# A hybrid attention and mLSTM encoder layer: another order of the attention unit's steps, and four more pieces of dense products at the start of each attention stage

## The chip, the core and the metric

The kernel runs on one NeuronCore of a Trainium2 chip. A core has a matrix engine (TensorE, "PE" in the profile; its weight loads are "PEld"), VectorE ("DVE"), ScalarE ("ACT"), GpSimd ("POOL") and SyncE ("SP"), which here mostly issues DMAs. Each engine works through its own instructions in order and waits on semaphores for the others. The metric is device time in microseconds (us) of one execution of the whole program. The kernel before takes 2937.11 us (median of 3 runs, 2936.93 to 2938.26).

## What is computed

One encoder layer over two sequences (1024 and 2048 tokens, each with 16 learned meta tokens in front), model width 1024, in 32-bit floating point:

```python
xn = _rmsnorm(h, g_pre)
proj = xn @ w_in + b_in                      # 1024 -> 6672 columns
na_q, na_k, na_v, na_z, ml_qk, ml_v, ml_z, ml_o, ml_g, mg = jnp.split(proj, SPLIT_IDX, axis=-1)
ya = _neighbourhood_attention(...)           # 8 heads of 64, window of 8 rows x 16 columns, plus meta keys
ya = (ya * jax.nn.silu(na_z)) @ w_a
yb = (_mlstm_branch(...) * jax.nn.silu(ml_z)) @ w_b   # 4 heads of 128, both directions
ga, gb = jnp.split(jax.nn.sigmoid(mg), 2, axis=-1)
y = (ga * ya + gb * yb) @ w_out
return h + _rmsnorm(y, g_post)
```

In the neighbourhood attention each block of queries (8 rows by 16 columns, 128 queries) sees the keys of up to 15 rows by 32 columns and the meta keys; a bias table and a mask give each query its own window:

```python
s_win = jnp.einsum('bcqhd,bwckhd->bhcqwk', q_blk, k_blk) * scale
s_win = jnp.where(valid[:, :, None, :], s_win + bias, NEG)
s_met = jnp.einsum('bcqhd,bmhd->bhcqm', q_blk, km) * scale
p = jax.nn.softmax(jnp.concatenate([s_met, s_win], axis=-1), axis=-1)
```

## The kernel before

Large products are made of three products of 32-bit values cut into a high and a low half (high times high, high times low, low times high: `mm3`, lines 141 to 146). The cutting is work for ScalarE (the high half is a rounding copy) and VectorE (the low half is the difference); the text calls it splitting.

**Two streams.** `dense` is a generator for the input projection (`group`, lines 412 to 414 for the token-major columns, 144 to 146 for the feature-major ones), and for the six "finals" of 512 tokens each (`final`): the merge of the two branches with `w_a`, `w_b` (lines 144 to 146 on `yh`, `yl`) and `w_out` (lines 1304 to 1306). `sparse` is a generator for the rest: mLSTM of the first sequence, attention of the first sequence, mLSTM of the second, attention of the second. `run` weaves them: each `yield` of the sparse stream carries a cost (`A_NA` = 1.52 for attention), and `run` takes pieces from the dense stream until their costs (about 1.4 each: 12 matmuls of 256 columns or 6 of 512) have paid for it. So a `yield` in the sparse stream puts about one piece of dense products into TensorE's order. When the sparse stream has ended, the remaining pieces follow without anything between. A dense final for which an attention or mLSTM result is still missing may not start. There are 1642 pieces. The first attention stage begins at piece 449, the second at 1142 and ends at 1567; the last final begins at 1578.

TensorE's order is the order of this program text. The order on the other engines and of SyncE's DMA issues is chosen by a scheduler at build time.

**An attention stage** (`na`) walks over heads (a block of 8 rows, and one of 8 heads; 16 in the first stage, 32 in the second), and in each over 4 units `cb`, the blocks of 16 columns. For each unit there are four steps:

- `na_scores`: two matmuls on TensorE (lines 664, 665) into the one PSUM buffer `sc`; VectorE adds the bias and takes the maximum (668); ScalarE takes the exponential (672).
- `na_scale`: VectorE takes a reciprocal and scales the probabilities (680, 681), tile `prb`, 2 buffers.
- `na_turn`: four transposes on TensorE (689) into one of 2 PSUM buffers `tr`; ScalarE copies the high half (691), VectorE the low half (692), tile `pts`, 2 buffers.
- `na_out`: four matmuls with v on TensorE (701) into one of 2 PSUM buffers `sm`; ScalarE and VectorE add up the result (705, 707), and after the last unit of a pair of heads multiply it with the gate (709) and store it in HBM (710, tile `ya`).

These are spread over iterations of a loop: iteration `u` issues the scores of unit `u`, the product with v of unit `u - 2` and the transposes of unit `u - 1`, with a `yield` behind each.

`na_prep` loads and splits what the next head needs, in six parts: the DMA loads (`qr`, `kr`, `vr`, and so on, lines 550 and 629 to 633), then the splits of q (639, 641, 642), of k (644, 646) and of v (649, 651). In the loop these parts are called one by one between the steps. For the first head of a stage nothing runs ahead, so its six parts are called before the loop, with a `yield` behind each.

**The finals.** `yload` (lines 1245 to 1248) loads the eight pieces of 128 features of a final's input from HBM, four from attention (`ya`) and four from mLSTM (`yb`), through four buffers, and splits each (1247 on ScalarE, 1248 on VectorE). It is called in parts from the final before, as soon as the attention and mLSTM results are there; what is left of it is called at that final's end. The gates of the merge (`tg`, line 1267) are loaded for each block of features and multiplied on VectorE straight out of PSUM (1283, 1285), which sets free the accumulators `pj` (3 buffers). Weights come through four pairs of buffers, `whi` and `wlo` (line 231); the next pair's loads are issued when a pair is used up.

Of the kernel before, what the change touches and what calls it, by code (L numbers as in the profile page):

```python
# [48 lines left out]
def _row_types(R):  # L49

    out = []
    for t in range(R // 8):
        if t == 0:
            out.append((0, 0, 11))
        elif t == R // 8 - 1:
            out.append((2, R - 12, 12))
        else:
            out.append((1, 8 * t - 4, 15))
    return out
# [48 lines left out]
A_NA, A_D, A_A, A_N, A_G = 1.52, 1.63, 1.63, 1.85, 1.3  # L108


class K:
# [440 lines left out]
    def na(self, s, rts):  # L552

        tc, nc, i = self.tc, self.nc, self.i
        rows = _row_types(SEQLEN[s] // 64)
        with tc.tile_pool(name=f"na{s}{rts[0]}", bufs=1, side="right", reuse_waits="tile") as np_:
            self.qB = [np_.tile([P, 4, P], F32R, name=f"qB{j}") for j in range(2)]
            self.kx = [np_.tile([P, 16, 64], F32R, name=f"kx{j}") for j in range(2)]
            self.gts = [np_.tile([P, 17, 48], F32, name=f"gt{j}") for j in range(2)]
            for q in self.qB:  # L560
                nc.gpsimd.dma_start(q[64:128], i["onehot"].rearrange("a (b c) -> a b c", b=4))
            for g in self.gts:
                nc.gpsimd.memset(g[:, 0, :], 0.0)
                nc.gpsimd.memset(g[:, 16, :], 0.0)
            heads = [(rt, pr, hh) for rt in rts for pr in range(4) for hh in range(2)]
            n = len(heads)
            prep = self.na_prep(np_, s, rows, heads, 0)
            for k in range(6):
                next(prep, None)
                yield A_NA  # L570
            self.na_bias(rows, heads, 0)
            cur, nxt = self.head, None
            units = [(j, cb) for j in range(n) for cb in range(4)]
            ready = {}
            for u in range(len(units) + 2):
                if u < len(units):
                    j, cb = units[u]
                    if cb == 0:
                        cur = self.head
                        prep = self.na_prep(np_, s, rows, heads, j + 1) if j + 1 < n else iter(())  # L580
                        next(prep, None)
                    ready[u] = [cur, heads[j], cb, None, None, self.gts[j % 2]]
                    self.na_scores(np_, ready[u], rows)
                    if j + 1 < n and cb == 0:
                        self.na_bias(rows, heads, j + 1)
                yield A_NA
                if u < len(units):
                    self.na_scale(np_, ready[u])
                    if cb:
                        next(prep, None)  # L590
                if u >= 2:
                    self.na_out(np_, ready.pop(u - 2), s)
                yield A_NA
                if 1 <= u <= len(units):
                    self.na_turn(np_, ready[u - 1], rows)
                    if u < len(units) and cb >= 2:
                        next(prep, None)
                yield A_NA

    def na_bias(self, rows, heads, j):  # L600
# [892 lines left out]
```

## Time and profile before

| what | us |
|---|---|
| median of 3 runs | 2937.11 |
| profiled execution, device time | 2935.2 |
| its span, first to last instruction | 2933.4 |
| TensorE busy in the span | 2820.8 |
| first attention stage, first scores to last product with v | 794.6 to 1183.5 |
| second attention stage, likewise | 2024.5 to 2810.9 |
| last final, first matmul | 2829.5 |

All times in the text are counted from the start of the span. In the profile `out<-in` names the tiles that an instruction writes and reads, `x4` is a count, and a bracket at a line's end gives the idle time of the engine ahead of that instruction and what ended it. In tables of waits the three numbers are the total, how often, and the longest. In views by stretches each engine has its busy time and its number of instructions, and the last three columns are the granted clock of TensorE (1.00 is full), the busy share of the DMA engines and GB/s. In the chain of waits the columns are start, length and what ran.

### The profile page before, as it was taken

The page shows a single profiled execution, that of the slowest core. Times are in us where ns is not written, and L with a number is a line of the kernel's source. Part 1 is how long each engine was busy: PE and PEld are TensorE (multiplying, and loading weights), DVE is VectorE, ACT ScalarE, POOL GpSimd, SP SyncE. Part 2 cuts the span into 40 slices and gives each one's busy share as a digit, 9 for nine tenths or more (in the row PEclk, how much of TensorE's full clock was granted, in tenths as well). Part 3 has the DMA queues.
Part 4 walks back from the last instruction along what each step waited for, and adds up shares of the span by engine and source line. Part 5 has one row for each costly group of instructions (what it writes and reads, how often), then busy time and mean ns, then how long its engine had stood idle before and what let it go on. Part 6 is the DMA issues. An engine that isn't in the chain of part 4 may idle for free.

```text
span 2933.4 us, 49345 instructions
## 1 busy us (share of the span) xinstructions
PE 2820.8 (96%) x17488; PEld 2510.8 (86%) x17488; DVE 1747.6 (60%) x4722; ACT 1288.7 (44%) x3114; POOL 23.1 (1%) x107
## 2 busy tenths in 40 slices
PE   6999999999799999999999999989999999989998
PEld 6998898899689988888887998977888888879797
DVE  5233566556556665465568776565555557777843
ACT  4213546433344444456566554413444445435421
POOL 1000000000000000000000000000000000000000
PEclk9999999999899999999999999999999999999999
DMA  9655667656775654568679898488568658897875
GB/s 350 219 179 181 197 218 256 232 182 207 255 232 153 198 175 134 168 232 298 197 234 363 277 313 290 136 263 272 172 196 283 191 174 272 245 280 236 283 273 194
DMA packets 438760, 675.25 MB, mean 230 GB/s; under 512 B 52240, under 2 KB 253024, under 8 KB 438512
## 3 DMA queue, kind: packets, MB, share of 16 engines
q1 hardware_dynamic: 437392, 669.41, 70.1%
q0 software_dynamic: 1120, 2.69, 0.4%
q8 instruction: 137, 2.24, 0.3%
q14 instruction: 111, 0.91, 0.1%
HBM read 455.05 MB, written 216.90 MB: 229 GB/s over the span
## 4 chain that ended last, share of the span: by engine, by line
PE 83%; DMA 9%; DVE 5%; ACT 1%; issue 1%; SPq 1%; DVEq 0%; ACTq 0%
PE pj L144 15%; PE pj L145 15%; PE pj L146 15%; PE pj L412 6%; PE pj L413 6%; PE pj L414 6%; PE sm L701 3%; PE pj L1304 3%; PE pj L1306 3%; PE pj L1305 3%; PE tr L689 2%; DMA tg<-gt 2%; PE sc L665 1%; PE sc L664 1%; PE sm L146 1%; PE sm L145 1%
## 5 line engine op out<-in xcount | busy, mean ns | idle before, releaser
L144 PE MATMUL pj<-xh,whi 128*128 128x512 f32 (+1 forms) x1824 | 722.2, 396 | 2.4 <-DVE xl L310 2.2
L145 PE MATMUL pj<-xl,whi 128*128 128x512 f32 (+1 forms) x1824 | 701.3, 384 | 0.6 <-DVE xl L310 0.6
L146 PE MATMUL pj<-xh,wlo 128*128 128x512 f32 (+1 forms) x1824 | 699.8, 384 | 0.0
L412 PE MATMUL pj<-whi,xh 128*128 128x256 f32 (+3 forms) x1576 | 450.8, 286 | 0.0
L413 PE MATMUL pj<-wlo,xh 128*128 128x256 f32 (+3 forms) x1576 | 444.7, 282 | 0.0
L414 PE MATMUL pj<-whi,xl 128*128 128x256 f32 (+3 forms) x1576 | 444.2, 282 | 0.0
L146 PEld LDWEIGHTS pj<-xh,wlo 128*128 128x128 f32 x1824 | 344.6, 189 | 72.3
L144 PEld LDWEIGHTS pj<-xh,whi 128*128 128x128 f32 x1824 | 345.2, 189 | 57.3 <-DVE xl L310 2.6
L145 PEld LDWEIGHTS pj<-xl,whi 128*128 128x128 f32 x1824 | 345.9, 190 | 53.3 <-DVE xl L310 0.8
L412 PEld LDWEIGHTS pj<-whi,xh 128*128 128x128 f32 (+1 forms) x1576 | 294.3, 187 | 1.2
L413 PEld LDWEIGHTS pj<-wlo,xh 128*128 128x128 f32 (+1 forms) x1576 | 294.0, 187 | 1.1
L414 PEld LDWEIGHTS pj<-whi,xl 128*128 128x128 f32 (+1 forms) x1576 | 294.1, 187 | 0.9
L692 DVE TENSOR_TENSOR pts<-tr,pts 96x512 fp32r<-96x512 f32 (+2 forms) x192 | 132.2, 688 | 159.4 <-ACT pts L691 158.3
L672 ACT ACTIVATE prb<-sc,mx 128x384 f32<-128x384 f32 (+2 forms) x192 | 119.4, 622 | 238.2 <-DVE mx L668 234.1
L1304 PE MATMUL pj<-whi,mh 128*128 128x256 f32 x768 | 221.0, 288 | 0.4 <-DMA whi<-wh 0.4
L1306 PE MATMUL pj<-whi,mlo 128*128 128x256 f32 x768 | 217.6, 283 | 2.1 <-DVE mlo L1287 2.1
L1305 PE MATMUL pj<-wlo,mh 128*128 128x256 f32 x768 | 217.2, 283 | 0.0
L691 ACT ACTIVATE pts<-tr 96x512 fp32r<-96x512 f32 (+2 forms) x192 | 114.3, 595 | 170.0 <-PE tr L689 169.3
L421 DVE TENSOR_TENSOR stT<-pj,bb 128x256 f32<-128x256 f32 (+3 forms) x197 | 83.1, 422 | 145.3 <-PE pj L414 141.2
L144 PE MATMUL pj<-yh,whi 128*128 128x512 f32 x384 | 158.0, 412 | 11.0 <-DVE tg L1283 11.0
L668 DVE CUSTOM_DVE_ANT_1 sc<-sc,gt 128x384 f32<-128x384 f32 (+2 forms) x192 | 118.9, 619 | 73.2 <-PE sc L665 67.4
L146 PE MATMUL pj<-yh,wlo 128*128 128x512 f32 x384 | 153.4, 399 | 0.0
(234 smaller groups left out, 5067.5 us busy)
## 6 DMA issues: line engine op xcount, KB each, us to landing
whi<-wh SPq DMA_DIRECT2D x176, 512.0 KB
wlo<-wl SPq DMA_DIRECT2D x176, 512.0 KB
wh<-whi SPq DMA_DIRECT2D x64, 512.0 KB
wl<-wlo SPq DMA_DIRECT2D x64, 512.0 KB
wraw<-w_in SPq DMA_DIRECT2D x48, 512.0 KB
gt<-st SPq DMA_DIRECT2D x96, 256.0 KB
tg<-gt SPq DMA_DIRECT2D x96, 256.0 KB
xh<-xh SPq DMA_DIRECT2D x6, 2048.0 KB
```

The source lines that it names most:

```text
L144: mm(out, ah, bh, start=start, stop=False)
L145: mm(out, ah, bl, start=False, stop=False)
L146: mm(out, al, bh, start=False, stop=stop)
L412: nc.tensor.matmul(o, xh, wh, start=k == 0, stop=False)
L413: nc.tensor.matmul(o, xh, wl, start=False, stop=False)
L414: nc.tensor.matmul(o, xl, wh, start=False, stop=k == KT - 1)
L668: nc.vector.tensor_tensor_reduce(out=so, in0=so, in1=gt[:, g0:g0 + ns, c0:c0 + 32], op0=ALU.add, op1=ALU.min, scale=-1.0, scalar=3.0e38, a ...
L672: nc.scalar.activation(pr_[:, :N].rearrange("p (b a c) -> p b a c", b=4, c=8), sc[:, :N].rearrange("p (a b c) -> p b a c", b=4, c=8), AF.E ...
L692: nc.vector.tensor_tensor(pts[:ks, :, 1, :], pt[:ks], pts[:ks, :, 0, :].bitcast(F32), op=ALU.subtract)
L1304: nc.tensor.matmul(o, mh[:, k, xs], wh, start=k == 0, stop=False)
L1305: nc.tensor.matmul(o, mh[:, k, xs], wl, start=False, stop=False)
L1306: nc.tensor.matmul(o, ml[:, k, xs], wh, start=False, stop=k == KT - 1)
```

## The change

In the loop of `na`, the transposes of unit `u - 1` move from the third step to the second, ahead of whose `yield` they now stand, behind the scaling of unit `u`; the product with v of unit `u - 2` moves from the second step to the third. The second part of `na_prep` in an iteration keeps its place in the third step. The first of the six parts before the loop, the one with the loads, is followed by five `yield`s instead of one; this holds for both attention stages.

```diff
             for k in range(6):
                 next(prep, None)
-                yield A_NA
+                for _ in range(1 if k else 5):
+                    yield A_NA
...
                     self.na_scale(np_, ready[u])
                     if cb:
                         next(prep, None)
+                if 1 <= u <= len(units):
+                    self.na_turn(np_, ready[u - 1], rows)
+                yield A_NA
                 if u >= 2:
                     self.na_out(np_, ready.pop(u - 2), s)
-                yield A_NA
-                if 1 <= u <= len(units):
-                    self.na_turn(np_, ready[u - 1], rows)
-                    if u < len(units) and cb >= 2:
-                        next(prep, None)
+                if u < len(units) and cb >= 2:
+                    next(prep, None)
                 yield A_NA
```

With it the second attention stage begins at piece 1146 and ends at piece 1575 of the dense stream; the last final still begins at 1578. From line 571 on the changed kernel's lines stand one lower: line 701 is 702 there, and so on.

## The prediction

> **What bounds the kernel now.** I read the engines' shares first, then the waits of TensorE, then the stretches in which attention runs, then the queues around its two ends.
>
> ```profile
> span 2933.4 us, 49345 instructions
> PE 2820.8 (96%) x17488; PEld 2510.8 (86%) x17488; DVE 1747.6 (60%) x4722; ACT 1288.7 (44%) x3114; POOL 23.1 (1%) x107
> ```
>
> TensorE is the bound: it is busy for 2820.8 of 2933.4 us. The change issues the same matmuls, so only the 112.6 us in which TensorE stands still can shrink or grow. The table of TensorE's waits (total, times, longest) says which of them attention owns:
>
> ```profile
> PE sm L701 <- DVE pts L692: 15.7, 12, 4.7
> PE sc L664 <- ACT kd L644: 15.0, 2, 14.1
> ...
> PE pj L1304 <- DMA whi<-wh: 0.4, 1, 0.4
> ```
>
> L701 is the product with v, waiting for the second half of the split of the transposed probabilities. L664 is the first score of an attention stage, waiting for the split of its loads. The transposes (L689) never wait, as the groups by line show (the last column is idle time before them):
>
> ```profile
> L701 PE MATMUL sm<-pts,vt 96*128 96x256 f32 (+2 forms) x768 | 124.2, 284 | 16.0 <-DVE pts L692 15.7
> L689 PE MATMUL tr<-ident,prb 128*96 128x128 f32 (+2 forms) x768 | 115.8, 274 | 0.0
> ```
>
> **Part 1, the order within a unit step.** Between two steps TensorE gets a piece of dense products. An undisturbed stretch of the chain of waits gives its length:
>
> ```profile
> 2539.98 0.44 PE tr L689 x4
> ...
> 2541.87 0.23 PE sc L664
> 2542.10 0.23 PE sc L665
> ...
> 2543.76 0.47 PE sm L701 x4
> ```
>
> From the end of the transposes (2540.42) to the scores are 1.45 us, from the scores' end (2542.33) to the product with v 1.43 us. So a piece is 1.43 us, scores take 0.46, transposes 0.44, the product with v 0.47. Before, a unit's transposes stand two pieces ahead of its product with v: 2 x 1.43 + 0.44 + 0.46 = 3.8 us. After, four pieces: 4 x 1.43 + 0.44 + 0.47 + 0.46 + 0.44 = 7.5 us. The price is paid by the other handoff: from scores to the same unit's transposes it was five pieces with scores, two products, transposes and scores between, 5 x 1.43 + 2.3 = 9.5 us; it becomes four pieces and one product fewer, 7.6 us. Lead is moved from a handoff that never waits to the one that does.
>
> Where the waits of L701 lie, in the tables of TensorE's waits for the first attention stage (760 to 1190 us) and then the second (2005 to 2830 us):
>
> ```profile
> PE sm L701 <- DVE pts L692: 1.4, 2, 0.8
> ...
> PE sm L701 <- DVE pts L692: 14.3, 10, 4.7
> PE pj L144 <- DVE tg L1283: 6.1, 3, 5.2
> PE sc L664 <- ACT kd L644: 0.9, 1, 0.9
> PE sc L665 <- DVE kx L646: 0.5, 1, 0.5
> ```
>
> The early 1.4 us are short (0.8 at most) and go: -1.4. The 14.3 us lie where the final products run beside attention. The worst place, in the timeline:
>
> ```profile
> 2520.22 0.74 PE L701 MATMUL sm<-pts,vt 128*128 128x256 f32 x4 [1.11 <-DVE pts L692]
> 2520.80 0.60 PE L689 MATMUL tr<-ident,prb 128*128 128x128 f32 x4
> ...
> 2523.38 0.40 PE L664 MATMUL sc<-kd,stk 128*128 128x512 f32 x1
> ...
> 2527.81 1.35 DVE L1248 TENSOR_TENSOR yl<-yr,yh 128x512 fp32r<-128x512 f32 x2 [6.85 <-ACT yh L1247]
> ...
> 2530.13 1.22 PE L701 MATMUL sm<-pts,vt 128*128 128x256 f32 x4 [4.70 <-DVE pts L692]
> 2533.29 0.49 DVE L681 TENSOR_SCALAR prb<-prb,sm 128x512 f32<-128x512 f32 x1
> ```
>
> VectorE's queue stands for 6.85 us behind a load that the split of the next final's input needs (L1248), and everything queued behind it is late: first the split of the transposes of 2520.80, for which L701 waits until 2530.13, then the scaling (L681, done 2533.8) of the scores of 2523.38. In the new order with VectorE's times as they are, the product is due at 2520.80 + 7.5 = 2528.3 and waits 1.8 us; the transposes of those scores are due at 2523.38 + 7.6 + 1.8 = 2532.8 and wait 1.0. That is 2.8 us where it was 1.11 + 4.70 = 5.8: half is gained, half turns up at the transposes. What holds VectorE in that stretch (2480 to 2780 us):
>
> ```profile
> DVE tg L1283 <- DMA tg<-gt: 13.7, 11, 4.7
> ...
> DVE yl L1248 <- ACT yh L1247: 9.4, 2, 6.9
> ...
> DVE yo L1376 <- DMA xres<-x_sample: 3.2, 2, 2.2
> ```
>
> These 26.3 us are late loads, which the new order doesn't hurry. I take half of the 14.3 us: -7. Upper bound, all of it. Lower bound, a loss: if each late microsecond of VectorE reached TensorE, 26.3 instead of the 14.3 + 6.1 = 20.4 of now, +5.9. I stay nearer the gain, because one worked place gives a half.
>
> After a wait the granted clock falls, as two rows behind waits of 4.7 and 2.5 us show:
>
> ```profile
> 2528.00:2535.00 7.00, 4.87 (x24) 4.87 (x25) 6.70 (x17) 5.14 (x16) 0.00 (x0) 0.53 0.74 214
> ...
> 2605.68 0.74 PE L701 MATMUL sm<-pts,vt 128*128 128x256 f32 x4 [2.47 <-DVE pts L692]
> ...
> 2606.00:2610.00 4.00, 4.00 (x16) 3.25 (x15) 2.96 (x9) 1.69 (x5) 0.00 (x0) 0.57 0.94 308
> ```
>
> The clock (0.53 and 0.57) cost 4.87 x 0.47 = 2.3 and 4.00 x 0.43 = 1.7 us. Since a 2.5 us wait is enough, waits of 1.8 and 1.0 us close together may still cost it; I count 0, and 4.0 as the bound.
>
> [...]
>
> **Part 2, four more pieces behind the first loads.** At the first attention stage the loads land late and TensorE runs dry:
>
> ```profile
> 781.44 10.67 DMA qr<-nq
> ...
> 794.59 0.69 PE L664 MATMUL sc<-kd,stk 128*128 128x384 f32 x1 [14.11 <-ACT kd L644]
> ...
> 795.00:800.00 5.00, 4.70 (x12) 3.56 (x12) 1.81 (x3) 1.15 (x2) 0.00 (x0) 0.50 1.02 368
> ...
> 803.82 0.23 PE pj L144
> ...
> 805.91 0.23 PE pj L144
> ```
>
> The four pieces are 24 matmuls of 512 columns here; nine take 805.91 - 803.82 = 2.09 us, so 24 take 5.6. The loads stand at the same place in SyncE's order, so the scores still start near 794.6 and the hole shrinks from 14.1 to 8.5 us: -5.6. Two of the pieces belong to the next group of columns, whose weights must have landed; TensorE waits for weights in 0.4 us of the whole run (above), so I take all four; if not, 2.8. The half clock after the hole (0.50, 4.70 x 0.5 = 2.4 us) stays, with 2.4 as a bound. At the second stage 0.9 + 0.5 us of waits are covered: -1.4.
>
> These pieces aren't new work, they are taken from the end. That is the price. The last product with v now stands nearer to the last final, which needs its result. In the built programs' order 156 matmuls lie between them before, 48 after.
>
> ```profile
> 2810.47 0.47 PE sm L701 x4
> ...
> 2814.64 0.32 SPq L1245 DMA_DIRECT2D yr<-ya  x1
> ...
> 2817.30 0.63 ACT L1247 ACTIVATE yh<-yr 128x512 fp32r<-128x512 f32 x1 [1.56 <-DMA yr<-ya]
> ...
> 2819.09 0.55 SPq L1245 DMA_DIRECT2D yr<-yb  x1
> ...
> 2827.23 0.63 ACT L1247 ACTIVATE yh<-yr 128x512 fp32r<-128x512 f32 x1 [2.94 <-DMA yr<-yb]
> ...
> 2829.49 0.23 PE pj L144
> ...
> 2829.52 0.32 SPq L231 DMA_DIRECT2D whi<-wh  x1
> ```
>
> Before, the final starts 18.5 us after that product, and the last input piece (yr<-yb) is on chip 2.3 us ahead. After, the final (call its start S) comes 48 x 0.12 = 5.8 us behind it (0.12: a piece of 1.43 has 12). SyncE's new order puts the last three yr<-yb loads behind the fourth pair of the final's weights, whose first issue was at S + 0.03 (2829.52). So they go out near S + 1 to S + 2, land 2.7 us later (2814.64 to 2817.30) to 8.1 us later (2819.09 to 2827.23), and take 0.63 + 0.68 = 1.3 us to split (L1247, half of L1248's 1.35). The eighth piece is then ready between S + 6 and S + 11.4; TensorE wants it after 21 matmuls of 0.23, at S + 4.8. So it waits 1.2 to 6.6 us, and up to 3.3 more for the clock (7 us at 0.53). Weights stood ahead of the 8.1 us load too, so I go toward that end: +5.
>
> **Sum.** -5.6 - 1.4 - 1.4 - 7 + 5 = -10.4 us: a span of 2923.0 and a profiled run near 2924.8, since the profiled run now takes 2935.2 for its span of 2933.4. The median of the runs shown, 2937.1, is 1.9 above that run; moved by the same amount it becomes 2926.7.
>
> **The rivals.**
> - The late split is forgotten altogether: VectorE catches up within 7.5 us everywhere and the clock stays up. For it: the transposes never wait now. Against it: 26.3 us of late loads. -5.6 - 1.4 - 1.4 - 14.3 - 4.0 + 5 = -21.7, 2915.4.
> - The order does nothing, the wait only moves: what L701 loses, L689 or the accumulators of L144 take up. For it: the second half of the place worked above; L144 already waits 6.1 us for VectorE. -5.6 - 1.4 - 1.4 + 5 = -3.4, 2933.7.
> - Slower: in the last stretch VectorE's in-order queue is the true bound, down to the last final, whose input it must split. Every late load of it reaches TensorE (+5.9) and the last handoff costs its upper end (6.6 + 3.3 = 9.9): -8.4 + 5.9 + 9.9 = +7.4, 2944.5. It turns the sign once that queue costs more than 8.4 us over now. Against it: VectorE is busy 60% and the transposes have 9.5 us of lead today.
>
> **How the numbers follow.** Forecast 0.45, everything forgotten 0.20, only moved 0.22, slower 0.13. The forecast's own range is 2920 to 2933. The instructions of VectorE, ScalarE and SyncE are reordered over the second half of the program, which moves small waits both ways, so the range goes from 2913 to 2941. A change under 0.2% (5.9 us) can't be told from none. Faster than 2931.2: most of the first (0.42), the second, 0.03 of the third, 0.65. Within: 0.03 + 0.19 + 0.03 = 0.25. Slower than 2943: 0.10.
>
> **What would show it.** Right: L664's longest wait near 8.5 us; L701 under 4 us in total; some 3 to 7 us of new waits at L689, where there were none; a new wait of about 5 us for yh or yl at the start of the last final. Wrong: L664 still waits 14 us (the loads or weights came later); L689 waits more than 14 us; the last final waits not at all or above 10 us; or a change in the mLSTM stages, which issue the same work, outweighs all of these.

## The result, and the profile after

The changed kernel takes 2922.68 us (median of 20 runs, 2917.26 to 2931.32) where the kernel before takes 2934.23 us (20 runs beside them, 2923.88 to 2938.26). The medians are 11.6 us apart. The ratio that is used from here on is reckoned from all the executions and not from the medians: 0.9968, with a 95% interval of 0.9959 to 0.9977, about 9.4 us faster. The forecast was 10.4 us faster. The two profiled executions differ by 8.3 us of span, and the working below goes by those.

First the engines' shares of the changed kernel:

```profile
span 2925.1 us, 49552 instructions
PE 2824.3 (97%) x17488; PEld 2514.2 (86%) x17488; DVE 1745.3 (60%) x4722; ACT 1287.4 (44%) x3114; POOL 23.0 (1%) x107
```

TensorE issues the same 17488 matmuls and is busy for 3.5 us more, so the gain is idle time: 100.8 us instead of 112.6. Its table of waits over the whole run:

```profile
...
PE sc L665 <- ACT kd L645: 10.6, 1, 10.6
PE tr L690 <- DVE prb L682: 9.8, 3, 6.4
...
PE pj L144 <- ACT yh L1248: 6.1, 3, 4.4
...
PE pj L1305 <- DVE yo L1333: 2.7, 1, 2.7
...
PE sm L702 <- DVE pts L693: 0.6, 1, 0.6
```

The product with v (L702, formerly L701) waits 0.6 us instead of 15.7. The transposes (L690), which never waited, now wait 9.8, and the last final's inputs (yh) 6.1. A product with w_out (L1305) waits 2.7 us for VectorE in the second attention stage, where these products did not wait before. The groups by line show the same exchange, in the last column:

```profile
L702 PE MATMUL sm<-pts,vt 96*128 96x256 f32 (+2 forms) x768 | 122.7, 282 | 0.6 <-DVE pts L693 0.6
L690 PE MATMUL tr<-ident,prb 128*96 128x128 f32 (+2 forms) x768 | 115.5, 273 | 9.8 <-DVE prb L682 9.8
```

An undisturbed stretch of the chain of waits (start, length, what ran) gives the new distances:

```profile
2542.30 0.44 PE tr L690 x4
...
2544.16 0.47 PE sm L702 x4
...
2547.96 0.44 PE tr L690 x4
...
2549.84 0.47 PE sm L702 x4
```

The transposes of 2542.30 have their product with v at 2549.84, 7.5 us later, as worked out; the product at 2544.16 is that of the unit before.

Where the 8.3 us between the two spans come from, stage by stage, by the starts of the same TensorE instructions in both traces. Four pieces (5.7 us at 1.43) have moved from the end of the second attention stage ahead of the first hole, and four more to that stage's own start; they are taken out of every difference.

| stretch | before | after | difference without the moved pieces |
|---|---|---|---|
| start to the first hole | 780.5 | 788.2 | +2.0 |
| the first hole | 14.1 | 10.6 | -3.5 |
| first attention scores to the second mLSTM's first gate product | 401.5 | 404.4 | +2.9 |
| second mLSTM, first gate product to first normalisation | 747.1 | 741.9 | -5.2 |
| from there to the second attention's first scores | 81.3 | 85.0 | -1.9 |
| second attention to the last final's first matmul | 804.8 | 780.3 | -13.1 |
| last final's first matmul to its first product with w_out | 48.8 | 59.3 | +10.5 |
| rest | 55.3 | 55.3 | 0.0 |

The first row is work that both kernels do alike. The stretch from 0 to 100 us had a granted clock of 0.98 in the profile of before and 0.95 in that of after; 77 us of matmuls times 0.03 are 2.3 us. Other kernels of this study have 0.95, 0.98 or 1.00 there, so this row stands for nothing that the change does on purpose.

The first hole, in TensorE's timeline and then in stretches of 5 us (clock, DMA share and GB/s are the last three columns):

```profile
798.86 0.69 PE L665 MATMUL sc<-kd,stk 128*128 128x384 f32 x1 [10.61 <-ACT kd L645]
```

```profile
790.00:795.00 5.00, 0.00 (x0) 0.00 (x0) 0.00 (x0) 0.00 (x0) 0.00 (x0) 0.83 0.76 217
795.00:800.00 5.00, 0.84 (x2) 0.45 (x2) 1.64 (x2) 2.10 (x3) 0.00 (x0) 0.50 0.67 160
800.00:805.00 5.00, 5.00 (x15) 4.06 (x16) 1.29 (x2) 1.34 (x3) 0.00 (x0) 0.64 1.00 379
```

The scores start at 798.86, 4.3 us later than before. Some 2 us of that is the first row of the table, the rest is a later split of the loads, so four pieces worth 5.6 us shortened the wait by 3.5 in this execution.

The last final, in TensorE's timeline, then SyncE's, then one stretch of 11 us:

```profile
2819.00 0.80 PE L144 MATMUL pj<-yh,whi 128*128 128x512 f32 x1 [4.45 <-ACT yh L1248]
2822.24 0.79 PE L144 MATMUL pj<-yh,whi 128*128 128x512 f32 x1 [1.29 <-ACT yh L1248]
```

```profile
2808.81 0.32 SPq L1246 DMA_DIRECT2D yr<-ya  x1
...
2811.12 0.42 SPq L1246 DMA_DIRECT2D yr<-yb  x1
2811.64 0.38 SPq L231 DMA_DIRECT2D whi<-wh  x1
2812.06 0.43 SPq L231 DMA_DIRECT2D wlo<-wl  x1
2812.53 2.99 SPq L1246 DMA_DIRECT2D yr<-yb  x3
```

```profile
2818.00:2829.00 11.00, 8.71 (x21) 5.88 (x22) 5.73 (x9) 2.52 (x4) 0.00 (x0) 0.56 0.75 257
```

The final starts at 2810.46, and its last four inputs (yr<-yb) are asked for at 2811.12 and from 2812.53 on. They are mLSTM results that had been in HBM for some 800 us; in SyncE's order they merely stand behind the attention piece (yr<-ya), which can't go before its result is stored, and behind weights. TensorE waits 6.3 us for inputs in all: 4.45 of them for the first of the four, asked for at 2811.12 and split from 2818.3 on, and 1.29 for the next. The mean clock of the stretch is 0.56.

### The profile page after: what moved, and what is told of

It is laid out like the page before. It is cut to its first block, busy times and chain, and to the rows that moved or that the text cites. A ratio compares the mean times of both kernels' runs of the same rounds, so it can differ in the third digit from the quotient of the medians.

```text
span 2925.1 us, 49552 instructions
## 1 busy us (share of the span) xinstructions
PE 2824.3 (97%) x17488; PEld 2514.2 (86%) x17488; DVE 1745.3 (60%) x4722; ACT 1287.4 (44%) x3114; POOL 23.0 (1%) x107
## 4 chain that ended last, share of the span: by engine, by line
PE 82%; DMA 9%; DVE 5%; ACT 1%; SPq 1%; issue 1%; ACTq 0%; DVEq 0%
PE pj L144 14%; PE pj L145 14%; PE pj L146 14%; PE pj L412 6%; PE pj L413 6%; PE pj L414 6%; PE pj L1305 3%; PE pj L1307 3%; PE pj L1306 3%; PE sm L702 3%; PE tr L690 3%; DMA tg<-gt 1%; PE sc L665 1%; PE sc L666 1%; PE sm L146 1%; DMA um<-ud 1%
## 5 line engine op out<-in xcount | busy, mean ns | idle before, releaser
L144 PE MATMUL pj<-xh,whi 128*128 128x512 f32 (+1 forms) x1824 | 722.3, 396 | 1.0 <-DVE xl L310 1.0
L144 PEld LDWEIGHTS pj<-xh,whi 128*128 128x128 f32 x1824 | 346.0, 190 | 55.9 <-DVE xl L310 1.2
L1305 PE MATMUL pj<-whi,mh 128*128 128x256 f32 x768 | 221.7, 289 | 2.7 <-DVE yo L1333 2.7
L708 DVE TENSOR_TENSOR yg<-sm,yg 64x128 f32<-64x128 f32 x384 | 108.4, 282 | 108.0 <-ACT yg L706 100.2
L144 PE MATMUL pj<-yh,whi 128*128 128x512 f32 x384 | 158.3, 412 | 8.5 <-ACT yh L1248 6.1
L145 PE MATMUL pj<-yl,whi 128*128 128x512 f32 x384 | 153.9, 401 | 0.2 <-DVE yl L1249 0.2
```

Of the source, the lines that this page charges most:

```text
L144: mm(out, ah, bh, start=start, stop=False)
L145: mm(out, ah, bl, start=False, stop=False)
L1305: nc.tensor.matmul(o, mh[:, k, xs], wh, start=k == 0, stop=False)
```

## The experiments

Every ratio is against the kernel before, from runs on the same chip. The other columns come from one profile of each kernel. "Hole" is the longest wait of the first stage's scores, "norm" the second mLSTM stage as in the table above, "attention" the second attention stage's difference to before, without moved pieces, and "final" the last final up to w_out.

| kernel | ratio (95%) | hole | norm | attention | final |
|---|---|---|---|---|---|
| before | 1 | 14.1 | 747.1 | 0 | 48.8 |
| after | 0.9968 (0.9959 to 0.9977) | 10.6 | 741.9 | -13.1 | 59.3 |
| e1_order | 0.9975 (0.9963 to 0.9987) | 15.2 | 745.5 | -10.9 | 50.0 |
| e2_pieces | 1.0007 (0.9993 to 1.0022) | 9.2 | 741.3 | +5.3 | 58.7 |
| e3_first | 0.9957 (0.9940 to 0.9974) | 10.5 | 743.0 | -8.4 | 51.3 |
| e4_early | 0.9965 (0.9953 to 0.9978) | 8.9 | 742.2 | +0.9 | 50.7 |
| e5_yb_first | 0.9935 (0.9917 to 0.9952) | 10.4 | 742.8 | -6.1 | 46.9 |
| e6_out_later | 0.9997 (0.9985 to 1.0010) | 14.5 | 746.2 | -7.4 | 48.6 |
| e7_yb_nine | 0.9954 (0.9937 to 0.9972) | 1.1 | 741.6 | +2.2 | 47.7 |
| e8_yb_before | 1.0010 (0.9999 to 1.0020) | 14.5 | 751.6 | -4.2 | 47.3 |
| e9_yb_pieces | 0.9987 (0.9975 to 0.9999) | 9.6 | 742.5 | +7.1 | 49.5 |
| e10_shift | 0.9962 (0.9948 to 0.9976) | 14.0 | 743.8 | -8.8 | 51.5 |
| e11_yb_order | 0.9977 (0.9966 to 0.9989) | 14.8 | 746.4 | -4.4 | 49.4 |
| e12_yb_first_stage | 0.9949 (0.9929 to 0.9969) | 9.3 | 742.5 | -9.9 | 49.3 |

A single profile of the same kernel can lie several us off its median (the runs of before reach from 2920 to 2944 us, those of after from 2917 to 2931). The profiled executions of after, e4_early and e11_yb_order are 4.4 to 4.7 us above their kernels' medians, that of e2_pieces 6.0. So a stage's difference of 2 or 3 us says little, and one of 5 us between two kernels can still be the execution's; the ratios decide.

**e1_order: the new order alone.** The changed kernel with one `yield` behind the loads, as before.

```diff
-                for _ in range(1 if k else 5):
+                for _ in range(1):
                     yield A_NA
```

> The new order of the steps alone: one yield behind the first loads, as before, so the second attention stage ends at piece 1567 again and 12 pieces (about 17 us) stand between the last product with v and the last final. Theory (each part adds up by itself: the order wins about 13 us beside the finals, the four pieces win about 5 at the two starts and lose about 10 at the last final): waits of the product with v under 4 us, transposes wait some 6 to 12 us, the first scores of the first stage wait about 14 us again, no wait for yh at the last final; ratio to before near 0.996, about as fast as both parts together. Rival 1 (the gain lies elsewhere: the mLSTM transposes L1205, whose wait fell from 15.9 to 7.3 us because the dense pieces are shifted by four against the mLSTM): without the shift L1205 waits about 16 us again, ratio 0.998 to 1.001. Rival 2 (the order only moves waits from the product with v to the transposes): ratio 0.999 to 1.002.

Measured 2924.45 against 2932.21 us. In its table of TensorE's waits:

```profile
...
PE sc L665 <- ACT kd L645: 15.4, 2, 15.2
...
PE tr L690 <- DVE prb L682: 6.2, 3, 2.8
```

The product with v is no longer among the first waits, the hole is back, and the last final costs 1.2 us more than before instead of 10.5. The order by itself is worth 0.25% here, less than the 0.4% expected of it.

**e2_pieces: the four pieces alone.** The kernel before with

```diff
-                yield A_NA
+                for _ in range(1 if k else 5):
+                    yield A_NA
```

> The four more pieces alone, in the order of the steps of before. Theory: the first scores of the first attention stage wait 10 to 11 us as in the changed kernel, the product with v waits about 14 us in all beside the finals as before, and the last final waits 4 to 6 us for yh and then runs some 10 us at half clock; -3.5 - 1.4 + 10 = about +5 us, ratio near 1.002. Rival 1 (gain from the shift against the mLSTM): L1204 waits 7 us instead of 16, ratio 0.997 to 1.000. Rival 2 (the pieces carry the whole gain): ratio near 0.997, as both parts together.

Measured 2933.99 against 2932.21 us. From 2005 us on TensorE waits:

```profile
PE sm L702 <- DVE pts L693: 22.6, 12, 3.5
PE pj L144 <- ACT yh L1248: 5.2, 2, 4.4
```

The hole shrinks to 9.2 us and the mLSTM stage is 5.8 us shorter, but the last final costs 9.9 us more, and L702 waits 22.6 us instead of 14.3. So the pieces alone win nothing, and the wait of the last final is theirs: it comes without the new order too.

**e3_first: the four pieces at the first stage only,** with the new order.

```diff
-                for _ in range(1 if k else 5):
+                for _ in range(5 if k == 0 and s == 0 else 1):
```

> The new order, and the four more pieces in the first attention stage only, so that the second stage ends at piece 1571 and eight pieces (about 11.5 us) stand between the last product with v and the last final instead of four. Theory: the last final's wait for yh falls from 6 us to between 0 and 2 and its half clock goes with it, 6 to 10 us are won against the changed kernel; the second stage's start waits about 1.4 us again; ratio to before near 0.994. Rival (the last final's wait isn't set by its distance to the last product with v, but by the weights ahead in SyncE's queue): the wait stays at 4 to 6 us, ratio 0.997.

Measured 2919.19 against 2932.21 us, where a ratio near 0.994 was expected. The attention ends four pieces earlier, the last final waits 2.0 us for yh instead of 6.1, and takes 51.3 us. The second stage's four pieces bought 0.9 + 0.5 us of waits and cost up to 8 at the other end; the whole kernel shows it only weakly (0.9957, intervals overlap with the change's).

**e4_early: the attention stream ends early.** The changed kernel with a smaller cost per step in the second stage, so that it takes fewer pieces between two steps and ends sooner.

```diff
+        cost = A_NA if s == 0 else 1.48
...
-                    yield A_NA
+                    yield cost
```

> The changed kernel with the cost of a step lowered from 1.52 to 1.48 in the second attention stage, so that its steps take fewer dense pieces and it ends at piece 1564 instead of 1575: about 15 pieces (21 us) between the last product with v and the last final. Theory: no wait for yh at the last final and full clock behind it, about 10 us won there; beside the finals a step's lead shrinks by 3%, which costs 0 to 3 us; ratio to before near 0.993. Rival (the wait for yh comes from weights and loads on SyncE's queue, wherever the product with v stands): ratio 0.997. Second rival (fewer pieces between steps make transposes and products wait more than the last final gains): the transposes wait over 16 us, ratio above 0.997.

Measured 2924.12 against 2932.21 us, a ratio of 0.9965 where 0.993 was expected. The last final falls to 50.7 us, but the gain is lost again inside the attention stage, where the scores now wait as well (1.4 us for the same cause in the changed kernel):

```profile
...
PE sc L666 <- ACT prb L674: 8.9, 6, 3.0
...
PE tr L691 <- DVE prb L683: 8.5, 5, 3.4
```

That the thinner weave is the cause is argued, not shown: this is one execution, and the transposes wait less than in the changed kernel (8.5 us against 9.8), far from the 16 us that the expectation asked for.

**e5_yb_first: the mLSTM pieces first.** The changed kernel, but `yload` fetches and `final` uses the four mLSTM pieces ahead of the four attention pieces.

```diff
-        for k in range(KT + 2):
+        ks = (4, 5, 6, 7, 0, 1, 2, 3)
+        for j in range(KT + 2):
...
-            for br in range(2):
+            for br in (1, 0):
...
-                if br:
+                if not br:
```

> The changed kernel, but every final loads and splits the four mLSTM pieces of its input first and the four attention pieces last, and multiplies in that order (w_b before w_a). The loads that don't depend on attention can then go out before the last product with v is done; behind it only the last attention piece is left. Theory (the last final waited because its last three loads stood behind weights in SyncE's queue, after the product with v): from the first matmul of the last final to its first product with w_out it takes 49 to 52 us as before the change (48.8), not 59.3; no wait for yh above 2 us there; 7 to 10 us less than the changed kernel, ratio to before 0.993 to 0.995. Rival (the write of the last attention piece and its load back set the wait, whichever pieces go first): the wait stays at 4 us or more, ratio near 0.997.

Measured 2916.52 against 2933.11 us, the best of the study. From 2805 us on this is all that TensorE waits for:

```profile
PE pj L144 <- DVE tg L1287: 2.0, 2, 1.2
```

No wait for yh is left and the final takes 46.9 us: the 10.5 us of the last final come from the order in which its inputs are asked for, as SyncE's rows above say.

**e6_out_later: lead for both handoffs.** The kernel before with the product with v one whole iteration later, so that the transposes keep their distance and the product gains five pieces.

```diff
-            for u in range(len(units) + 2):
+            for u in range(len(units) + 3):
...
-                if u >= 2:
-                    self.na_out(np_, ready.pop(u - 2), s)
+                if u >= 3:
+                    self.na_out(np_, ready.pop(u - 3), s)
```

> The kernel before, without the four pieces and with its order of steps, but with the product with v one whole iteration later (unit u - 3 instead of u - 2): five pieces between a unit's transposes and its product, and still five between its scores and its transposes. Theory (leads decide: a wait comes where VectorE's lateness exceeds the lead, and the changed order had to give up 1.9 us of lead at the transposes): beside the finals neither the transposes (0 to 3 us) nor the products with v (under 3 us) wait, the second attention stage up to the last final is 11 to 16 us shorter than before; some 2 us are lost at the last final (seven pieces behind the last product); ratio 0.995 to 0.997. Rival (the late loads of VectorE reach TensorE whatever the leads are): the same waits turn up at the scores, at L144 or at the w_out products, ratio 0.998 or above.

Measured 2933.59 against 2933.11 us. From 2000 us on:

```profile
PE sc L664 <- ACT prb L672: 6.4, 4, 2.6
...
PE tr L689 <- DVE sm L680: 3.9, 1, 3.9
PE tr L689 <- DVE prb L681: 3.0, 3, 2.3
```

The wait of L701 is gone altogether. But now the scores wait, whose one buffer `sc` isn't free, and the transposes, which wait with five pieces of lead. So it came as the rival has it: more lead at one handoff moved the wait to the next. The extra iteration also adds three `yield`s to each stage, so this kernel displaces the second mLSTM by three pieces. The hole, the mLSTM stage and the last final are those of before within 1 us; the stage's -7.4 us is not in the ratio. Two waits outside that column have grown: that of the second stage's first scores (0.9 to 4.1 us) and that of the mLSTM's gate product, L753 (2.9 to 6.2 us).

**e7_yb_nine: nine pieces at the first stage,** on top of e5_yb_first, none added at the second.

```diff
-                for _ in range(1 if k else 5):
+                for _ in range(9 if k == 0 and s == 0 else 1):
```

> As the run with the mLSTM pieces first, with nine yields behind the loads of the first attention stage instead of five, and one behind those of the second; the second stage ends at piece 1575 as in the changed kernel. Theory (the hole at the first scores is filled piece by piece): the first scores of the first stage wait 5 to 6 us instead of 10.6, with less half clock behind them; 3 to 6 us less than the run with five; 1 to 2 us more at the second stage's start; ratio to before 0.991 to 0.994. Rival (the loads come later by what the pieces fill, because their weights and stores compete for the DMA queues): the wait stays at 8 us or more and nothing is gained.

Measured 2921.93 against 2933.11 us, a ratio of 0.9954 where 0.991 to 0.994 was expected. TensorE's waits from 740 to 1195 us begin:

```profile
PE pj L146 <- DMA wlo<-wl: 1.6, 1, 1.6
PE pj L144 <- DMA whi<-wh: 1.2, 1, 1.2
PE sc L665 <- ACT kd L645: 1.1, 1, 1.1
```

The hole is all but filled (1.1 us instead of 10.4 with five), but the pieces ahead of it now wait 2.8 us for their weights. The kernel is still no faster than e5_yb_first. In the profiles the second attention stage is 8 us worse; its first scores wait 3.7 us there, and scores wait 12.8 us for ScalarE in the whole run. It runs the same pieces at the same displacement of eight, so it isn't the weave on TensorE that differs, but what the other queues did, or the one execution that was profiled.

**e8_yb_before and e9_yb_pieces: the mLSTM pieces first, in the old order of steps.** The edit of e5_yb_first in the kernel before (e8) and in e2_pieces (e9).

> The kernel before with the mLSTM pieces first in every final and nothing else. Theory (that edit only takes away the wait of a last final that stands close behind attention, and before it stands 13 pieces behind): same as before, ratio 0.999 to 1.001, 48 to 49 us from the last final's first matmul to its first product with w_out. Rival (loading the mLSTM pieces early helps every final, and the gain of the earlier run had nothing to do with the four pieces): ratio 0.996 to 0.998.

> The four more pieces in the order of steps of before, with the mLSTM pieces first. Theory (the pieces win about 5 us at the first hole and some 4 in the second sequence's mLSTM, and alone they gave that back at the last final): no wait for yh at the last final, 47 to 50 us there instead of 58.7, ratio to before 0.996 to 0.998. Rival (the pieces are worth nothing even without that wait): ratio 0.999 to 1.001.

Measured 2937.22 and 2932.33 against 2935.74 us. By itself the edit is worth nothing, since nothing waits there before. With the pieces it takes the last final from 58.7 to 49.5 us, and the pieces come out at 0.9987 instead of 1.0007. That is short of the 0.996 to 0.998 that was expected and as the rival had it: in the old order the pieces are worth little even when the last final waits for nothing.

**e10_shift: only a shift.** The kernel before with four pieces at the end of the first attention stage, where they cover nothing; the second stage is displaced by four pieces against the dense stream.

```diff
+            for _ in range(4 if s == 0 else 0):
+                yield A_NA
```

> The kernel before with four more yields behind the last step of the first attention stage, where they cover nothing: they only shift the dense stream by four pieces against the second sequence's mLSTM. Theory (that mLSTM stage is shorter in the changed kernel by the shift alone: 742 instead of 747 us from its first gate product to its first normalisation transposes): 741 to 744 us here too, the first scores still wait 14 us, eight pieces' distance at the end costs 2 us; ratio 0.998 to 1.000. Rival (the stage is shorter for another reason: the new order of steps, or by chance of a run): 745 to 748 us.

Measured 2921.29 against 2935.74 us: 0.9962, as much as the whole change. The hole is 14.0 us, as before, and the order is the old one; the second mLSTM is 3.3 us shorter, the second attention 8.8. Its waits from 2005 us on still lead with the product with v, at little less than before:

```profile
PE sm L703 <- DVE pts L694: 13.2, 12, 3.2
```

The worst single one is 3.2 instead of 4.7 us, and what has gone is the 6.1 us of L144 for the gates (0.6 here) and some half-clock time: the mean clock from 2025 to 2820 us is 1.00 here and 0.99 in the kernel before. The expectation had 0.998 to 1.000; the shorter mLSTM it foresaw, the shorter attention it did not.

**e11_yb_order: the new order with the mLSTM pieces first,** no pieces added.

> The new order of steps with the mLSTM pieces first, without the four pieces: with the three others of this kind it shows each part without the last final's wait. Theory (the parts add up): the second attention stage is 9 to 13 us shorter than before up to the last final, ratio 0.9955 to 0.9975, and the run with both parts is 5 to 9 us below it. Rival (the order alone carries the whole gain and the pieces only moved waits): ratio 0.9935, the same as with both.

Measured 2928.95 against 2935.74 us. Beside e8_yb_before, at the same displacement, the order leaves the second attention as it is (-4.4 and -4.2); the kernel is 0.33% faster all the same, by the profiles 5.2 us of it in the mLSTM stage, which neither kernel displaces. This misses the expectation twice: the attention is 4.4 us shorter than before where 9 to 13 were expected, and the kernel with both parts is 12 us ahead by the ratios where 5 to 9 were. So the parts don't simply add up.

**e12_yb_first_stage: e5_yb_first with the pieces at the first stage only.**

> The new order of steps, the four more pieces in the first attention stage only, and the mLSTM pieces first in every final. Theory (the hole of the first stage, the mLSTM stage's shift and the order's gain are kept, the last final waits for nothing): first scores wait 10 to 11 us, second mLSTM stage 741 to 744 us, last final 47 to 50 us to its first product with w_out, ratio 0.9925 to 0.9955. Rival (how the second attention stage's heads fall on the finals' loads decides as much as the order of steps, since a shift of four pieces alone won 11 us: this start, four pieces earlier than in the run with both, may fall worse): the second attention stage up to the last final is longer than 795 us and the ratio above 0.9965.

Measured 2916.73 against 2934.75 us. Level with e5_yb_first: once the handoff at the end costs nothing, the second stage's four pieces neither help nor hurt measurably.

## Why the prediction held

The sum, -10.4 us, was right to 1 us by the ratio and to 2.1 by the two profiles. That closeness is in good part luck. Against the table of stretches its terms were off by +2.1 (the hole), +4.3 (the early waits), -0.5, -6.1 (the order beside the finals) and +5.5 (the last final), and two stretches that it counted at nothing moved by -5.2 and +2.0. That is some 26 us of errors, which cancel to 2.1. The mechanisms of the hole, of the two handoffs and of the last final did appear where it put them. Point by point:

**The first hole, -5.6: short by about 2.** The longest wait is 10.6 us, not 8.5. Over the seven kernels with five `yield`s there it is 8.9 to 10.6 with a mean of 9.8, over the six with one it is 14.0 to 15.2 with a mean of 14.5: 4.7 us for 5.6 us of pieces. In this profile "the scores still start near 794.6" failed (798.86), but in the other six they start at 794.4 to 796.2, so that step holds to 1.6 us. The half clock behind the hole stayed, as counted (0.50 from 795 to 800 us, 0.64 in the 5 us behind). With e7_yb_nine the wait is 13.0 us shorter than before, and 10.2 if the new waits for weights are taken off, for 11.1 us of pieces. The prediction had taken late weights at nothing; for four pieces that was right, for eight it is not.

**The early waits of L701, -1.4: not seen in the time.** The waits went, but the first attention stage was 2.9 us longer in this profile.

**The start of the second stage, -1.4: measured -1.9.** The two waits of 0.9 and 0.5 us are gone. The row itself is within what single profiles scatter.

**The order beside the finals, -7: measured -13.1.** The mechanism was the one worked out, but it carries less than a third of the result: L702 lost 13.7 of its 14.3 us, and L690 gained 9.8 where 3 to 7 were foreseen. At the two handoffs that is -3.9, where -7 was counted. The largest of the new waits is exactly the kind of place that the prediction used, a late load at the head of VectorE's queue. TensorE's row and VectorE's:

```profile
2589.35 1.08 PE L690 MATMUL tr<-ident,prb 128*128 128x128 f32 x4 [6.45 <-DVE prb L682]
```

```profile
2583.27 0.75 DVE L1377 SCALAR_TENSOR_TENSOR yo<-yo,nwy,xres 128x512 f32<-128x512 f32 x1 [4.57 <-DMA xres<-x_sample]
```

VectorE stands 4.6 us for the residual's load, works off what is queued behind it, and scales `prb` only at 2588.7; the transposes, with their lead cut to 7.6 us, wait 6.45. What the sum did not have is the rest. The wait of L144 for the gates left this stage (6.1 us before; in the last final it is 2.1 us, where before has 2.8), and the wait of 2.7 us at L1305 came in. The stage as a whole stands so, before (to 2829.5, 0.2 us into the last final) and then after:

```profile
2024.50:2829.50 805.00, 783.81 (x4437) 677.16 (x4438) 511.99 (x1224) 372.26 (x847) 2.04 (x4) 0.99 0.75 233
```

```profile
2030.20:2810.50 780.30, 765.97 (x4384) 665.44 (x4383) 504.45 (x1216) 363.08 (x838) 2.05 (x4) 0.99 0.75 235
```

TensorE idles 14.3 us instead of 21.2, and is busy for 17.8 us less, of which the eight moved pieces are 11.4. The other 6.4 us are matmuls that took less time. The clock explains only part of them: by the traces' clock records this stage has 17.1 us at half clock before and 13.7 after, worth 1.7 us at most, where the prediction counted 0 and bounded it by 4.0. Where the rest comes from is not shown. The failed step is "I take half of the 14.3 us", a size from one worked place: 9.8 of the 13.7 us turned up at the transposes, and what made up for it, at L144 and in the matmuls, was not in the sum. And the size isn't fixed by the order. New order against old at the same displacement, in the second attention stage of one profile each and in the ratios of all executions:

| pair | pieces of displacement | length of the stage, us | TensorE's idle time in it, us | whole kernel, by the ratios |
|---|---|---|---|---|
| e1 against before | 0 | -10.9 | -7.5 | -0.25% |
| e11 against e8 (mLSTM pieces first) | 0 | -0.2 | -0.3 | -0.33% |
| e3 against e10 | 4 | +0.4 | -2.8 | -0.05% |
| after against e2 | 8 | -18.4 | -10.7 | -0.39% |
| e5 against e9 (mLSTM pieces first) | 8 | -13.2 | -7.5 | -0.52% |

The idle time falls in all five pairs. The five differences in length reach from +0.4 to -18.4 us, with a mean of -8.5; the ratios are all on the same side, with a mean of 0.31%, 9 us. What makes the size is not the order alone. e10_shift, which only displaces the stage, moved it by 8.8 us. Nor is it the displacement alone: after, e5 and e7 have the same order and the same eight pieces, and stand at -13.1, -6.1 and +2.2. Two causes are left. Each edit also gives VectorE's and SyncE's queues a new order at build time, and which late load meets which handoff changes with it. And each figure of a stage rests on one execution of each kernel, while executions of one kernel lie up to 14 us apart (after: 2917.26 to 2931.32). By the ratios the order is worth 1.5 to 15 us in the five pairs, each uncertain by some 3.5 to 6.5 us by the intervals above, so little of that scatter is sure. The runs don't separate the two causes.

**The last final, +5: measured +10.5.** The mechanism was right: 5.7 us from the end of the last product with v to the final (5.8 foreseen), the mLSTM pieces behind the weights in SyncE's queue, and 6.3 us of waits where 1.2 to 6.6 were bounded. One part of the working was not: it put the wait at the eighth piece, behind the last three loads. The longest wait, 4.45 us, is for the fifth, whose load went out only at 2811.12, behind another pair of weights, and was on chip 7.2 us later. The failed step in the sum is the choice "+5" and with it "up to 3.3 more for the clock": the stretch from 2818 to 2829 has 8.71 us of matmuls at 0.56, so the clock cost 8.71 x 0.44 = 3.8 us by the prediction's own way of reckoning. The upper end of the range, 9.9, was the right value. e5_yb_first shows the cause by removing it, and e2_pieces that it belongs to the pieces.

**The second mLSTM stage, 0: measured -5.2.** The prediction named this only as a way to be wrong. TensorE's waits from 1195 to 2005 us, before and then after:

```profile
PE tr L1204 <- DVE hn L1193: 10.0, 1, 10.0
```

```profile
...
PE tr L1205 <- DVE hn L1194: 2.0, 1, 2.0
```

All nine kernels that displace this stage by four or eight pieces need 741.3 to 743.8 us for its stretch, and the four that don't displace it 745.5 to 751.6. e6_out_later, which displaces it by three, needs 746.2. The longest wait for `hn` there goes the same way: 7.9 to 10.0 us without displacement, 5.2 with three pieces (the row below), 2.0 to 3.0 with four or eight. e10_shift is among the nine, with nothing but the displacement. That it is the displacement, with the queue orders that the build makes for it, is shown; why VectorE's normalisation is late in the one and not in the other was not pursued.

```profile
PE tr L1204 <- DVE hn L1193: 5.2, 1, 5.2
```

**The rivals.** "Forgotten altogether" fails by the 9.8 us at L690. "Only moved" fails by e1_order, whose interval (0.9963 to 0.9987) lies below 1 without any pieces, and by the idle time that falls in all five pairs. The ratio of the whole change would not refute it, since a displacement alone gained as much, and e3 against e10 is a pair in which the kernel's time hardly changed. "Slower" has its place right (the last final did cost its upper end) and its first half wrong: the late loads didn't all reach TensorE.

**What stays open.** e1_order alone is worth 0.25% and e2_pieces alone nothing, together they make 0.32%; with intervals of 0.1% each this is near additive, but part of every one of these figures is how the collisions fell in that build, and the runs can't split it off. The order's own worth is about 9 us by both means of the five pairs, with a scatter of 8 us in the stage's length, of which the executions make up an unknown part.

## What to carry to other kernels

When two independent streams are woven into one engine's order, any edit that moves one against the other by a few pieces also changes which late load meets which handoff. Here a displacement alone was worth as much (e10_shift, 0.9962) as the whole change (0.9968), while another kernel with displacement and the old order gained nothing (e2_pieces, 1.0007). Run a pure shift as a control before crediting a reordering, and compare stages over several executions. Pieces of cover taken from the end of a stream have their price at its last handoff: look at what queue the final consumer's loads stand in, and load first what has long been ready. That small edit is worth nothing alone (1.0010), and with it the change came out twice as good (0.9935 instead of 0.9968).

## What the runs showed of the hardware

In the last final the half clock of TensorE lasted longer than the waits it came with. The waits are of 4.45 and 1.29 us, with 2 us of work between them; by the trace's clock record the clock was halved from 2817.45 to 2827.69, 10.24 us. From 2823.55 to 2827.39 matmuls of 512 columns came every 0.43 us, where every 0.23 us was the pace before the waits and after. TensorE's timeline:

```profile
2823.98 0.63 PE L144 MATMUL pj<-yh,whi 128*128 128x512 f32 x1
2824.41 0.63 PE L145 MATMUL pj<-yl,whi 128*128 128x512 f32 x1
...
2828.00 0.39 PE L145 MATMUL pj<-yl,whi 128*128 128x512 f32 x1
2828.23 0.40 PE L146 MATMUL pj<-yh,wlo 128*128 128x512 f32 x1
```

The later part of that stretch, and what follows it, by windows:

```profile
2820.87:2824.28 3.41, 2.12 (x5) 1.41 (x5) 2.06 (x4) 1.89 (x3) 0.00 (x0) 0.50 0.34 104
2824.28:2827.69 3.41, 3.41 (x9) 2.64 (x9) 2.15 (x3) 0.00 (x0) 0.00 (x0) 0.50 0.91 299
2827.69:2831.10 3.41, 3.41 (x16) 2.75 (x16) 2.90 (x5) 0.63 (x1) 0.00 (x0) 1.00 0.97 313
```

TensorE's timeline has no wait between 2822.24 and 2831, and the clock was back at 1.00 from 2827.69 on, 5.4 us later. In the traces of before and after, the 25 half-clock stretches that aren't cut off by the end of the run are 3.41, 6.83, 10.24 or 17.07 us long. One of 3.41 us follows the wait of 2.47 us in the profile before:

```profile
2602.91:2606.32 3.41, 0.94 (x7) 0.64 (x6) 3.18 (x8) 0.04 (x1) 0.00 (x0) 1.00 1.01 364
2606.32:2609.73 3.41, 3.41 (x12) 2.70 (x12) 2.37 (x6) 1.56 (x4) 0.00 (x0) 0.50 0.99 319
```
